# A two-layer decoder trunk on one core: SBUF homes at set distances modulo 512 bytes, and another order for the first stage

## The chip, the cores and the metric

The kernel runs on one core of a Trainium2 chip. The metric is device time in microseconds of one execution. Three runs of the kernel before took 998.0, 998.24 and 998.68 us.

## The reference

The input x is 256 positions by 1,024 channels, c is a conditioning vector, all in float32. Two layers, each of three residual sub-layers, and a final RMSNorm:

```python
def modnorm(x, g, shift, scale):
    return rmsnorm(x, g) * (1 + scale[:, None, :]) + shift[:, None, :]
def swiglu(h, w_gate, w_up, w_down):
    return (jax.nn.silu(h @ w_gate) * (h @ w_up)) @ w_down
c_act = jax.nn.silu(c)
for l in range(DEPTH):
    mod = (c_act @ w_mod[l] + b_mod[l]).reshape(B, N_SUB, 3, D_MODEL)
    shift, scale, gate = mod[:, :, 0], mod[:, :, 1], mod[:, :, 2]
    h = modnorm(x, norm_g[l, 0], shift[:, 0], scale[:, 0])
    x = x + 0.5 * gate[:, 0, None, :] * swiglu(h, w_ffn_gate[l, 0], w_ffn_up[l, 0], w_ffn_down[l, 0])
    h = modnorm(x, norm_g[l, 1], shift[:, 1], scale[:, 1])
    y = even_mixer(...) if l % 2 == 0 else odd_mixer(...)
    x = x + gate[:, 1, None, :] * y
    h = modnorm(x, norm_g[l, 2], shift[:, 2], scale[:, 2])
    x = x + 0.5 * gate[:, 2, None, :] * swiglu(h, w_ffn_gate[l, 1], w_ffn_up[l, 1], w_ffn_down[l, 1])
return rmsnorm(x, final_g)
```

The inner width of a SwiGLU is 2,816. The even mixer is a pooling mixer beside differential attention, the odd one a chunkwise mLSTM; each sits between one projection in and one out.

## The kernel before

Channels lie on the 128 partitions, so x is eight tiles `x[k]` of 128 x 256. All projections together are 2,560 units. A unit is one 128 x 128 block of a weight matrix times one 128 x 256 tile. For accuracy each weight block is split into a rounded high part `wh` and the rest `wl`, and each tile into a high and a low part. So a unit is three matmuls in a row (mm3, lines 341 to 343): `wh` with the high part, `wl` with the high part, `wh` with the low part.

**The weight stream.** SP loads chunks of 16 units (1 MB, `raww`) into five buffers that it shares with chunks `rawm` of the modulation matrix. For every half chunk ACT makes `wh` (line 299) and DVE makes `wl` by subtraction (line 300); four buffers each of `wh` and `wl`. A `rawm` chunk is read by DVE alone: `mod_sums` (line 267) multiplies it with silu(c) (`cact`) and sums along the row, two instructions of 128 x 1,024 a chunk. SP may load into a raw buffer again when DVE has read it.

**The moving operands** are three sets of tiles. In the first FFN, and for the first ten blocks of each later projection in, it is `xh[k]`/`xl[k]` (in the latter 258 columns, as two columns carry the shift); else `xs[k]`, the normed x. In the projections down and out it is a pair of tiles `hid`.

**The homes.** A tile's home is its address within the partition. The pools lay tiles one behind the other, each rounded up to 32 bytes. `xh`, `xl` and `hid` are 258 columns (1,032 bytes, so 1,056) and each next home lies 32 bytes further modulo 512; `xs` tiles are 1,024 bytes and all lie alike. Counted from the home of the weights (`wh` and `wl` all lie alike, a unit's columns at multiples of 512 bytes), modulo 512, worked out from the sizes: `xh[k]` at 320 + 32k, `xl[k]` at 64 + 32k, every `xs` at 320, the 46 `hid` slots at all sixteen multiples of 32.

**The first stage** (`first_ffn`, lines 526 to 597). DVE and ACT square the eight tiles, PE sums each over the partitions by matmuls with a column of ones (line 540), DVE makes the mean (`nv`, 543), POOL the power -1/2 (`nr`, 545), PE spreads it over the partitions (418). x times that (`hid`) is made by DVE for k = 0 (553) and by POOL for k = 1 to 7 (556). Then for each k the sixteen units of the first eight blocks follow (`START_BLOCKS`), for which DVE does the two modulation sums of k, the scale column (`acol`, 368), two `wl` and `xl[k]` (587), and ACT `xh[k]` (585) and a second copy in full precision (586). Behind its multiplications POOL makes masks and bands (`constants`, lines 208 to 235), which the mixers need later.

The order on each engine is made by a scheduler of the program, which takes instructions by when their inputs would be there; `issue_after` and `keep_in_program_order` bind single ones.

## Time and profile before

| | before |
|---|---|
| runs | 998.24 us median (998.0 to 998.68) |
| the profiled execution: time, span | 998.09 us, 996.4 us |
| PE busy, matmuls recorded | 973.5 us (98%), 8,032 |
| DVE, ACT, POOL busy | 758.1 us (76%), 528.0 us (53%), 217.9 us (22%) |
| DMA | 247.18 MB, mean 248 GB/s |
| granted clock, mean | 0.996 |

The span runs from the first to the last instruction. PE is matrix multiplication, PEld its weight loads, DVE, ACT and POOL the vector, scalar and general engines, SP the queue that issues the loads. Matmuls overlap in the pipeline, so their time is read from one start to the next and not from a record's length.

### The profile page before, as it was taken

To read this page: it belongs to the slowest core of one execution; us is meant where nothing else is said; L and a number is where in the kernel's file an instruction comes from. 1 tells how busy PE (TensorE), PEld (TensorE's weight loads), DVE (VectorE), ACT (ScalarE), POOL (GpSimd) and SP (SyncE) were. 2 spreads that over 40 slices of the span, in tenths; PEclk is the share of its full clock that TensorE was granted. 3 is DMA by queue.
4 is the path that set the end of the run, shared out by engine and by line. 5 is a ranking of instruction groups with operands and counts; after the bars stand their busy time and mean duration, and the time that the engine had idled before them with its cause. 6 is when DMAs were issued, how large, how long until landed. Compare 5 with 4: busy or idle time off the path is not lost.

```text
span 996.4 us, 19641 instructions
## 1 busy us (share of the span) xinstructions
PE 973.5 (98%) x8032; PEld 958.8 (96%) x8032; DVE 758.1 (76%) x1201; ACT 528.0 (53%) x872; POOL 217.9 (22%) x223
## 2 busy tenths in 40 slices
PE   7999999999999999999999999999999999999996
PEld 6899999999999999999999999999899999999996
DVE  5979998989879876777798676788867988555452
ACT  3475544448766544444465444445767655444441
POOL 4953220110112322211122222001010113222011
PEclk9999999999999999999999999999999999999998
DMA  9978888875846766766758766676565746565521
GB/s 341 317 295 318 328 329 319 341 284 206 298 155 246 271 245 254 277 252 235 290 182 291 288 245 248 269 293 258 200 223 185 280 171 244 205 229 175 187 105 43
DMA packets 36093, 247.18 MB, mean 248 GB/s; under 512 B 4001, under 2 KB 4385, under 8 KB 7458
## 3 DMA queue, kind: packets, MB, share of 16 engines
q1 hardware_dynamic: 35856, 245.81, 66.7%
q8 instruction: 63, 1.03, 0.4%
q14 instruction: 28, 0.23, 0.1%
q10 hardware_dynamic: 146, 0.11, 0.0%
HBM read 244.86 MB, written 1.05 MB: 247 GB/s over the span
## 4 chain that ended last, share of the span: by engine, by line
PE 82%; DVE 9%; ACT 3%; issue 3%; POOL 1%; DVEq 0%; ACTq 0%; POOLq 0%
PE one L343 26%; PE one L341 26%; PE one L342 26%; DVE wl L300 3%; DVE rawm L267 3%; ACT wh L299 1%; DVE xs L447 1%; POOL hr L401 1%; DVE xn L445 1%; PE one L418 0%; DVE xl L587 0%; DVE t L512 0%; DVE h L490 0%; ACT L488 0%; PE one L842 0%
## 5 line engine op out<-in xcount | busy, mean ns | idle before, releaser
L300 DVE TENSOR_TENSOR wl<-raww,wh 128x1024 fp32r<-128x1024 f32 x320 | 395.5, 1239 | 162.4 <-ACT wh L299 161.1
L299 ACT ACTIVATE wh<-raww 128x1024 fp32r<-128x1024 f32 x320 | 337.2, 1056 | 226.7 <-PE one L343 197.3
L341 PE MATMUL one<-xs,wh 128*128 128x256 f32 x976 | 275.3, 282 | 0.0
L342 PE MATMUL one<-xs,wl 128*128 128x256 f32 x976 | 272.9, 280 | 1.0 <-DVE wl L300 1.0
L343 PE MATMUL one<-xs,wh 128*128 128x256 f32 x976 | 273.1, 280 | 0.0
L341 PE MATMUL one<-hid,wh 128*128 128x256 f32 x832 | 233.7, 281 | 0.2 <-ACT hid L601 0.2
L343 PE MATMUL one<-hid,wh 128*128 128x256 f32 x832 | 233.7, 281 | 0.0
L342 PE MATMUL one<-hid,wl 128*128 128x256 f32 x832 | 233.3, 280 | 0.0
L342 PE MATMUL one<-xh,wl 128*128 128x258 f32 (+1 forms) x752 | 207.5, 285 | 3.2 <-DVE wl L300 2.9
L341 PE MATMUL one<-xh,wh 128*128 128x258 f32 (+1 forms) x752 | 208.1, 287 | 1.8 <-ACT xh L585 1.8
L343 PE MATMUL one<-xl,wh 128*128 128x258 f32 (+1 forms) x752 | 204.6, 283 | 0.0
L493 POOL TENSOR_TENSOR hid<-h,hid 128x256 fp32r<-128x256 f32 x88 | 123.3, 1402 | 340.1 <-ACT hid L492 340.1
L342 PEld LDWEIGHTS one<-xs,wl 128*128 128x128 f32 x976 | 183.6, 188 | 1.4 <-DVE wl L300 1.2
L341 PEld LDWEIGHTS one<-xs,wh 128*128 128x128 f32 x976 | 183.0, 187 | 1.2 <-issue 1.0
L343 PEld LDWEIGHTS one<-xs,wh 128*128 128x128 f32 x976 | 183.1, 188 | 0.0
L341 PEld LDWEIGHTS one<-hid,wh 128*128 128x128 f32 x832 | 156.8, 188 | 0.4 <-ACT hid L601 0.4
L343 PEld LDWEIGHTS one<-hid,wh 128*128 128x128 f32 x832 | 156.6, 188 | 0.2 <-DVE hid L602 0.2
L342 PEld LDWEIGHTS one<-hid,wl 128*128 128x128 f32 x832 | 156.7, 188 | 0.0
L267 DVE CUSTOM_DVE_ANT_0 rawm<-rawm,cact,pk 128x1024 f32<-128x1024 f32 x112 | 150.5, 1371 | 0.0
L342 PEld LDWEIGHTS one<-xh,wl 128*128 128x128 f32 x752 | 140.6, 191 | 5.4 <-DVE wl L300 5.2
L341 PEld LDWEIGHTS one<-xh,wh 128*128 128x128 f32 x752 | 140.3, 191 | 4.1 <-ACT xh L585 2.3
L343 PEld LDWEIGHTS one<-xl,wh 128*128 128x128 f32 x752 | 138.8, 189 | 0.2 <-DVE xl L587 0.2
(222 smaller groups left out, 727.0 us busy)
## 6 DMA issues: line engine op xcount, KB each, us to landing
...
```

The costliest lines, as they stand in the source:

```text
L267: nc.vector.tensor_tensor_reduce(out=ri, in0=ri, in1=cact, scale=factor, scalar=first, op0=ALU.mult, op1=ALU.add, accum_out=modc[n // KT][ ...
L299: nc.scalar.activation(whs[i], src, AF.Copy)
L300: ins = nc.vector.tensor_tensor(out=wls[i], in0=src, in1=whs[i].bitcast(F32), op=ALU.subtract)
L341: nc.tensor.matmul(out, lhsT=wh, rhs=rh, start=start, stop=False, skip_group_check=skip)
L342: nc.tensor.matmul(out, lhsT=wl, rhs=rh, start=False, stop=False, skip_group_check=skip)
L343: nc.tensor.matmul(out, lhsT=wh, rhs=rl, start=False, stop=stop, skip_group_check=skip)
L401: nc.gpsimd.tensor_tensor(out=r, in0=v, in1=mhalf[:, 0:width], op=ALU.pow)
L445: nc.vector.scalar_tensor_tensor(out=xn, in0=x[k], scalar=a, in1=r, op0=ALU.mult, op1=ALU.mult)
L447: nc.vector.scalar_tensor_tensor(out=to[1], in0=xn, scalar=b, in1=to[0].bitcast(F32), op0=ALU.add, op1=ALU.subtract)
L493: nc.gpsimd.tensor_tensor(out=hl[:, 0:T], in0=h, in1=hh[:, 0:T].bitcast(F32), op=ALU.subtract)
```

## The change

- **Homes.** The hid slots are 256 columns wide and come from two pools of 23, one for high parts (`slots()` takes one of each) and one for low parts; other users take turns. Fillers and the order of the tiles set the homes: weights at 0 modulo 512, high parts (`xs[k][0]`, first pool) at 448, low parts (`xs[k][1]`, second pool) at 192, `xh`/`xl` at 128, 160, 384 and 416, with `xl[k]` like `xh[k]`. Two users that need more than 256 columns (`gr`, `cp` in the odd mixer) take a buffer of the tag `acc`.
- **The first FFN uses `xs`** in all its units, not `xh`/`xl`.
- **Sums.** DVE squares k = 0, 1, 4 and ACT the other five; DVE adds them up in two sums of four; PE does four matmuls with ones instead of sixteen.
- **Order.** One modulation sum of k = 0 goes ahead of the mean, the other behind a copy of POOL's result. x times its norm goes from POOL to DVE in all k, with the scale in the same instruction; ACT makes only the high part (bias), DVE the low part. The matmuls of k = 0 go by operand: sixteen with `wh`, sixteen with `wl`, sixteen with the low part.
- **Matmuls of ones.** 21 matmuls of 128 x 256 whose result nobody reads: 8 ahead of the sums, 2 and 7 behind them, 4 behind the spreading. One SiLU of one column goes ahead on ACT.
- **POOL's constants** go piece by piece, from k = 0 on, bound only behind the power. The load of `pk2` stands behind them; `ghalf`, `gc` and `hg` are made behind the last x of the first stage.

```diff
+CONST_BASE = 16512
+RAW_PHASE, HIGH_PHASE, LOW_PHASE = 128, 448, 192
+SKIP = 192
...
-    hid = ctx.enter_context(tc.tile_pool(name="hid", bufs=46))
     tmp = ctx.enter_context(tc.tile_pool(name="tmp", bufs=2))
     small = ctx.enter_context(tc.tile_pool(name="small", bufs=2))
+    skip = ctx.enter_context(tc.tile_pool(name="skip", bufs=1))
+    hids = [ctx.enter_context(tc.tile_pool(name="hid0", bufs=23))]
+    skip2 = ctx.enter_context(tc.tile_pool(name="skip2", bufs=1))
+    hids.append(ctx.enter_context(tc.tile_pool(name="hid1", bufs=23)))
...
-    def slot(dt=F32):
-        return hid.tile([P, XC], dt, tag="hid", name=nm("hid"))
+    turn = [0]
+
+    def slot(dt=F32, i=None):
+
+        if i is None:
+            i = turn[0] = 1 - turn[0]
+        return hids[i].tile([P, T], dt, tag="hid", name=nm("hid"))
+
+    def slots():
+        return slot(F32R, 0), slot(F32R, 1)
...
+    modc, xh, xl = [], [], []
+    for i in range(2 * KT):
+        if i % 2 == 0:
+            up_to(RAW_PHASE, 256)
+        (xh if i < KT else xl).append(fixed(f"x{i}", XC, F32R))
+        if i % 2 == 1 and len(modc) < DEPTH * NSUB * 3:
+            modc += [fixed(f"mod{len(modc) + j}", KT) for j in range(6)]
+    mhalf = fixed("mhalf", 2)
+    wgh = fixed("wgh", 64, F32R)
+    up_to(HIGH_PHASE, 512)
+    xs = [[fixed(f"xs{k}", T, F32R)] for k in range(KT)]
+    wgl = fixed("wgl", 64, F32R)
+    up_to(LOW_PHASE, 512)
+    for k in range(KT):
+        xs[k].append(fixed(f"xs{k}l", T, F32R))
+    pk = fixed("pk", NPACK)
...
+    up_to(0, 512)
+    fill(skip, SKIP, "skip")
+    fill(skip2, (LOW_PHASE - HIGH_PHASE) % 512, "skip2")
...
+    onesr = xs[KT - 1][1]
+    nc.vector.tensor_copy(onesr, ones[:, 0:1].broadcast_to([P, T]))
+    junk = scol("junk", 1)
+    nc.scalar.activation(junk, ones[:, 0:1], AF.Silu)
+    warm = one()
+
+    def warm_up(n):
+
+        for _ in range(n):
+            tc.keep_in_program_order(nc.tensor.matmul(warm[:, 0:T], lhsT=onesr[:, 0:P], rhs=onesr, start=True,
+                                                         stop=True))
...
+    def constants_lane(behind):
+        for i, piece in enumerate(constants()):
+            with tc.issue_after(behind):
+                piece()
+            if i % 2:
+                yield 4
         nc.sync.dma_start(pk2, pack2)
+        yield 64
...
-        hh, hl = slot(F32R), slot(F32R)
+        hh, hl = slots()
...
+        acc, sq = [slot()[:, 0:T] for _ in range(2)], [slot()[:, 0:T] for _ in range(KT)]
+        for k in range(KT):
+            to = acc[0] if k == 0 else acc[1] if k == 4 else sq[k]
+            if k in (2, 3, 5, 6, 7):
+                nc.scalar.activation(to, x[k], AF.Square)
+            else:
+                nc.vector.tensor_tensor(out=to, in0=x[k], in1=x[k], op=ALU.mult)
+            if k % 4:
+                last = nc.vector.tensor_tensor(out=acc[k // 4], in0=acc[k // 4], in1=to, op=ALU.add)
+                tc.keep_in_program_order(last)
+        warm_up(8)
         pss = one()
-        for k in range(KT):
-            sq = slot()
-            if k in (5, 6, 7):
-                nc.scalar.activation(sq[:, 0:T], x[k], AF.Square)
-            else:
-                nc.vector.tensor_tensor(out=sq[:, 0:T], in0=x[k], in1=x[k], op=ALU.mult)
+        for j, v in enumerate(acc):
             for i in range(2):
-                nc.tensor.matmul(pss[:, i:i + 1], lhsT=sq[:, i * P:(i + 1) * P], rhs=ones[:, 0:1],
-                                 start=k == 0 and i == 0, stop=k == KT - 1, skip_group_check=True)
+                tc.keep_in_program_order(
+                    nc.tensor.matmul(pss[:, i:i + 1], lhsT=v[:, i * P:(i + 1) * P], rhs=ones[:, 0:1],
+                                     start=j == 0 and i == 0, stop=j == 1, skip_group_check=True))
+            warm_up((2, 7)[j])
         v = scol("nv", 2)
+        with tc.issue_after(last.ins):
+            mod_sums(0, 1)
         nv = nc.vector.tensor_scalar(out=v, in0=pss[:, 0:2], scalar1=1.0 / D, scalar2=EPS, op0=ALU.mult, op1=ALU.add)
+        tc.keep_in_program_order(nv)
         stat["rcol"] = scol("nr", 2)
-        nc.gpsimd.tensor_tensor(out=stat["rcol"], in0=v, in1=mhalf, op=ALU.pow)
-        with tc.issue_after(nv.ins):
+        pw = nc.gpsimd.tensor_tensor(out=stat["rcol"], in0=v, in1=mhalf, op=ALU.pow)
+        after = nc.vector.tensor_copy(scol("after", 2), stat["rcol"])
+        tc.keep_in_program_order(after)
+        with tc.issue_after(after.ins):
             mod_sums(0)
-            nc.vector.tensor_scalar(out=ghalf, in0=pcol("b_mod", 0, 144), scalar1=0.5, scalar2=None, op0=ALU.mult)
         psb = stats_bcast()
-        for k in range(KT):
-            xn.append(slot()[:, 0:T])
-            if k == 0:
-                nc.vector.tensor_tensor(out=xn[k], in0=x[k], in1=psb, op=ALU.mult)
-                nc.scalar.activation(rext[:, 0:T], psb, AF.Copy)
-            else:
-                last = nc.gpsimd.tensor_tensor(out=xn[k], in0=x[k], in1=rext[:, 0:T], op=ALU.mult)
+        warm_up(4)
...
-            nc.scalar.activation(xh[k][:, 0:T], xn[k], AF.Identity, bias=b, scale=a)
-            nc.scalar.activation(xn[k], xn[k], AF.Identity, bias=b, scale=a)
-            nc.vector.tensor_tensor(out=xl[k][:, 0:T], in0=xn[k], in1=xh[k][:, 0:T].bitcast(F32), op=ALU.subtract)
+            xn.append(slot()[:, 0:T])
+            if k == 0:
+                for i in range(2):
+                    high(i)
+            xi = nc.vector.scalar_tensor_tensor(out=xn[k], in0=x[k], scalar=a, in1=psb if k == 0 else rext[:, 0:T],
+                                                op0=ALU.mult, op1=ALU.mult)
+            xc = nc.scalar.activation(xs[k][0], xn[k], AF.Identity, bias=b)
+            if k == 0:
+                tc.keep_in_program_order(xc)
+                tc.keep_in_program_order(nc.scalar.activation(rext[:, 0:T], psb, AF.Copy))
+                with tc.issue_after(xi.ins):
+                    split_to(1)
+            nc.vector.scalar_tensor_tensor(out=xs[k][1], in0=xn[k], scalar=b, in1=xs[k][0].bitcast(F32),
+                                           op0=ALU.add, op1=ALU.subtract)
             split_to(((k + 1) * nb - 1) // HALF_UNITS)
+            if k == 0:
+                ws = [(out(b), unit(), b) for b, _ in order[0:nb]]
+                for j in range(3):
+                    for o, (wh, wl), b in ws:
+                        tc.keep_in_program_order(
+                            nc.tensor.matmul(o, lhsT=wl if j == 1 else wh, rhs=xs[0][j // 2],
+                                             start=j == 0 and b[1] == 0, stop=False, skip_group_check=True))
+                spawn(constants_lane(pw.ins))
+                continue
             for b, _ in order[k * nb:(k + 1) * nb]:
-                mm3(out(b), (xh[k][:, 0:T], xl[k][:, 0:T]), k == 0 and b[1] == 0, k == KT - 1, True)
+                mm3(out(b), xs[k], False, k == KT - 1, True)
                 if k == KT - 1:
                     done(b)
         look[0] = 2
-        with tc.issue_after(last.ins):
-            constants()
-        gemm(order[KT * nb:], range(KT), lambda k: (xh[k][:, 0:T], xl[k][:, 0:T]), out, done)
+        with tc.issue_after(xi.ins):
+            nc.vector.tensor_scalar(out=ghalf, in0=pcol("b_mod", 0, 144), scalar1=0.5, scalar2=None, op0=ALU.mult)
+            nc.vector.tensor_scalar(out=gc, in0=pcol("subln_g"), scalar1=1.0 - LAMBDA_INIT, scalar2=None, op0=ALU.mult)
+            nc.vector.tensor_scalar(out=hg, in0=pcol("mlstm_g", 0, 8), scalar1=0.5, scalar2=None, op0=ALU.mult)
+        gemm(order[KT * nb:], range(KT), lambda k: xs[k], out, done)
...
-            gr = slot()
+            gr = tmp.tile([P, XC], F32, tag="acc", name=nm("gr"))
...
-            cp = slot()
+            cp = tmp.tile([P, XC], F32, tag="acc", name=nm("cp"))
```

**DVE from the mean to the first weights.** `nv` is the mean, `rawm`/`mod` a modulation sum, `hid` x times its norm, `acol` the scale column, `wl` the low weights. Before:

```order
L543 TENSOR_SCALAR nv_202<-one_169 128x2 [waits PE_49]
L267 ISA rawm_163,mod_120<-rawm_163,cact,pk 128x1024 [waits DMAHW4_49,Activation_49]
L267 ISA mod_120 128x1
L267 ISA rawm_163,mod_121<-rawm_163,cact,pk 128x1024 [waits DMAHW5_49]
L267 ISA mod_121 128x1
L548 TENSOR_SCALAR ghalf<-pk 128x144
L553 TENSOR_TENSOR hid_212<-xa,one_209 128x256 [waits PE_49]
L368 SCALAR_TENSOR_TENSOR acol_229<-mod_121,pk 128x1 [waits DVE_49]
L300 TENSOR_TENSOR wl_235<-raww_166,wh_234 128x1024 [waits DMAHW6_49,Activation_49]
```

Now:

```order
L340 ISA rawm_186,mod_90<-rawm_186,cact,pk 128x1024 [waits DMAHW4_49,DMAHW2_49]
L340 ISA mod_90 128x1
L632 TENSOR_SCALAR nv_238<-one_224 128x2 [waits PE_49]
L636 COPY after_243<-nr_241 128x2 [waits Pool_49]
L340 ISA rawm_186,mod_91<-rawm_186,cact,pk 128x1024 [waits DMAHW5_49]
L340 ISA mod_91 128x1
L447 SCALAR_TENSOR_TENSOR acol_253<-mod_91,pk 128x1 [waits DVE_49]
L674 SCALAR_TENSOR_TENSOR hid_255<-xa,acol_253,one_246 128x256 [waits DVE_49,PE_49]
L379 TENSOR_TENSOR wl_263<-raww_189,wh_256 128x1024 [waits DMAHW6_49,Activation_49]
```

One sum moved ahead of `nv`; the other waits for POOL's power (through the copy), and `hid` now waits for `acol`, as the scale is in it.

**DVE in one k of the first stage**, here from `acol` of k = 1 to the next sum. Before:

```order
L368 SCALAR_TENSOR_TENSOR acol_229<-mod_121,pk 128x1 [waits DVE_49]
L300 TENSOR_TENSOR wl_310<-raww_302,wh_309 128x1024 [waits DMAHW1_49,Activation_49]
L300 TENSOR_TENSOR wl_314<-raww_302,wh_313 128x1024 [waits DMAHW2_49,Activation_49]
L587 TENSOR_TENSOR xl_92<-hid_215,xh_84 128x256 [waits Activation_49]
L267 ISA rawm_365,mod_120<-rawm_365,cact,pk 128x1024 [waits DMAHW3_49]
```

Now:

```order
L447 SCALAR_TENSOR_TENSOR acol_253<-mod_91,pk 128x1 [waits DVE_49]
L379 TENSOR_TENSOR wl_343<-raww_333,wh_341 128x1024 [waits DMAHW1_49,Activation_49]
L674 SCALAR_TENSOR_TENSOR hid_337<-xa,acol_253,rext 128x256 [waits DVE_49]
L379 TENSOR_TENSOR wl_347<-raww_333,wh_345 128x1024 [waits DMAHW2_49,Activation_49]
L682 SCALAR_TENSOR_TENSOR xs1l<-hid_337,mod_90,xs_130 128x256 [waits Activation_49]
L340 ISA rawm_407,mod_90<-rawm_407,cact,pk 128x1024 [waits DMAHW3_49]
```

DVE has one instruction more, `hid`, and it stands behind the first `wl`. Not seen here: on ACT both `wh` of a k now stand ahead of its high part, where before the high part stood between them.

**POOL behind the power** (`nr`). Before:

```order
L545 TENSOR_TENSOR nr_204<-nv_202,mhalf 128x2 [waits DVE_49]
L556 TENSOR_TENSOR hid_215<-xa,rext 128x256 [waits DMAHW1_49,Activation_49]
L556 TENSOR_TENSOR hid_217<-xa,rext 128x256
L556 TENSOR_TENSOR hid_219<-xa,rext 128x256
L556 TENSOR_TENSOR hid_221<-xa,rext 128x256 [waits DMAHW3_49]
L556 TENSOR_TENSOR hid_223<-xa,rext 128x256
L556 TENSOR_TENSOR hid_225<-xa,rext 128x256
L556 TENSOR_TENSOR hid_227<-xa,rext 128x256
L210 MEMSET m_831 128x384
```

Now:

```order
L635 TENSOR_TENSOR nr_241<-nv_238,mhalf 128x2 [waits DVE_49]
L275 MEMSET m_324 128x384
L281 CAST identr<-ident 128x128 [waits Pool_49]
L277 AFFINE_SELECT m_324<-m_324 128x128 [waits Pool_49]
L277 AFFINE_SELECT m_324<-m_324 128x128
```

The seven multiplications are gone, and the pieces of the constants follow the power in the same order as before, with no other work of POOL between them.

## Rows read from the trace of the kernel before

**Rows 1.** The page, part 1: engine, busy us (share of the span), instructions.

```profile
PE 973.5 (98%) x8032; PEld 958.8 (96%) x8032; DVE 758.1 (76%) x1201; ACT 528.0 (53%) x872; POOL 217.9 (22%) x223
```

**Rows 2.** Busy us of engines by stretch, clock granted, DMA share, GB/s.

```profile
0.00:25.00 25.00, 19.20 (x86) 16.12 (x87) 13.07 (x27) 7.70 (x12) 10.21 (x13) 1.00 0.90 340
25.00:50.00 25.00, 23.76 (x186) 22.50 (x186) 23.02 (x34) 11.98 (x16) 25.00 (x41) 1.00 0.93 319
100.00:200.00 100.00, 100.00 (x849) 100.00 (x849) 89.08 (x134) 48.39 (x67) 17.40 (x15) 1.00 0.86 330
```

**Rows 3.** The timeline to the first units: start us, us, engine, line, operation [idle before].

```profile
5.02 1.43 DVE L538 TENSOR_TENSOR hid<-xa 128x256 f32<-128x256 f32 x4 [3.82 <-DMA xa<-xT]
...
5.99 6.99 PE L540 MATMUL one<-ones,hid 128*128 128x1 f32 x32
...
6.59 1.02 ACT L536 ACTIVATE hid<-xa 128x256 f32<-128x256 f32 x3
...
13.01 0.16 DVE L543 TENSOR_SCALAR nv<-one 128x2 f32<-128x2 f32 x1 [5.78 <-PE one L540]
...
13.26 1.73 POOL L545 TENSOR_TENSOR nr<-nv,mhalf 128x2 f32<-128x2 f32 x1 [11.89 <-DVE nv L543]
...
16.30 0.42 DVE L553 TENSOR_TENSOR hid<-xa,one 128x256 f32<-128x256 f32 x1 [0.51 <-PE one L418]
...
17.68 1.01 PE L341 MATMUL one<-xh,wh 128*128 128x256 f32 x3 [1.42 <-ACT xh L585]
```

**Rows 4.** The same timeline: POOL, and a DVE sum beside it.

```profile
17.22 9.66 POOL L556 TENSOR_TENSOR hid<-xa,rext 128x256 f32<-128x256 f32 x7 [2.23 <-ACT rext L554]
...
21.09 1.75 DVE L267 CUSTOM_DVE_ANT_0 rawm<-rawm,cact,pk 128x1024 f32<-128x1024 f32 x1
...
26.82 0.41 POOL L210 MEMSET m<- 128x384 f32 x1
...
56.24 1.92 POOL L232 TENSOR_TENSOR band<-band,ident 128x128 f32<-128x128 f32 x2
```

**Rows 5.** The timeline of the first stage at k = 1 and around k = 7.

```profile
24.57 0.58 DVE L368 SCALAR_TENSOR_TENSOR acol<-mod,pk 128x1 f32<-128x1 f32 x1
...
25.24 0.60 ACT L585 ACTIVATE xh<-hid,mod,acol 128x256 fp32r<-128x256 f32 x1 [5.23 <-DVE acol L368]
...
25.90 0.38 PE L341 MATMUL one<-xh,wh 128*128 128x256 f32 x1 [0.43 <-ACT xh L585]
...
57.96 1.28 DVE L300 TENSOR_TENSOR wl<-raww,wh 128x1024 fp32r<-128x1024 f32 x1 [0.55 <-ACT wh L299]
59.16 0.45 DVE L587 TENSOR_TENSOR xl<-hid,xh 128x256 fp32r<-128x256 f32 x1
59.54 1.34 DVE L267 CUSTOM_DVE_ANT_0 rawm<-rawm,cact,pk 128x1024 f32<-128x1024 f32 x1
...
62.13 0.16 DVE L368 SCALAR_TENSOR_TENSOR acol<-mod,pk 128x1 f32<-128x1 f32 x1
...
63.73 0.52 PE L341 MATMUL one<-xh,wh 128*128 128x256 f32 x3
```

**Rows 6.** PE alone by stretch: length, busy us (matmuls that reach into it), clock, DMA.

```profile
332.93:428.69 95.76, 95.76 (x815) 1.00 0.72 268
428.80:491.02 62.22, 62.22 (x530) 1.00 0.67 254
73.91:150.23 76.32, 76.32 (x647) 1.00 0.85 323
310.70:331.31 20.61, 20.61 (x174) 1.00 0.58 204
47.50:50.33 2.83, 2.83 (x26) 1.00 1.04 405
34.93:40.08 5.15, 5.15 (x44) 1.00 0.98 366
```

**Rows 7.** PE's timeline at a unit with `xh[4]` in the first FFN.

```profile
94.97 0.28 PE L341 MATMUL one<-xh,wh 128*128 128x256 f32 x1
...
95.32 0.28 PE L341 MATMUL one<-xh,wh 128*128 128x256 f32 x1
```

More of the change, by code (lines that the diff above doesn't have):

```diff
@@ L188, in pcol @@
+    identr = fixed("identr", P, F32R)
+    maskT = fixed("maskT", P)
+    tri = fixed("tri", P)
+    band = fixed("band", len(WINDOWS) * 3 * P, shape=[P, len(WINDOWS), 3 * P])
+    up_to(0, 512)
+    fill(skip, SKIP, "skip")
+    fill(skip2, (LOW_PHASE - HIGH_PHASE) % 512, "skip2")
     def pcol(n, i=0, w=1):
@@ L270, in mod_sums @@
                 mod_ready[n] = True
+            if sums is not None:
+                return
     mod_ready = {}
@@ L637, in even_mixer @@
         lamc = scol("lamc", 4)
-        gc = scol("gc")
         parts, vT, ys = {}, {}, {}
```

111 lines of the change are left out of this document (59 added, 52 removed).

## The prediction

> **What bounds the kernel now.** I read the page first: PE is busy 98% of the span [rows 1]. That alone doesn't say that PE is the limit everywhere, so the stretches come next. From 100 us on PE never pauses: 100.00 of 100 us, at full clock, with DVE at 89% and the loads at 330 GB/s [rows 2]. There only two things can shorten the run: fewer matmuls, or a shorter time from one matmul's start to the next. In the first 50 us it is otherwise: PE starts its first unit at 17.68 [rows 3], and from then to the end of the first stage it pauses for others. So the run is the time until PE no longer waits, plus about 7,700 matmuls at their spacing, plus what the mixers and the tail cost, which the change leaves alone.
>
> *Who holds PE in the first stage.* Up to the first unit it is a chain: squares from 5.02, 32 passes of PE with a column of ones that take 6.99 us, the mean at 13.01, POOL's power for 1.73, the spreading, x times it at 16.30, ACT, and PE at 17.68 [rows 3]. Then every k is one lap of DVE. `acol` stands at 24.57 for k = 1 and at 62.13 for k = 7 [rows 5]: six laps in 37.56 us, 6.26 each, in which DVE is busy 92% [rows 2]. PE needs 48 matmuls x 0.118 = 5.65 us a lap, so DVE, not PE, sets the pace. What DVE idles in a lap, it waits for ACT's `wh` (0.55 us) [rows 5]. The loads reach 319 to 340 GB/s there [rows 2]; SP's next load waits for a buffer that DVE gives back, so it follows DVE.
>
> *The spacing.* Taking off the one or two matmuls that reach into a stretch from before it, rows 6 give, in ns from start to start: `xs` 95.76 us over 813 = 117.8; `hid` 62.22 over 527 = 118.1; `xh`/`xl` in the first FFN 76.32 over 645 = 118.3; those of 258 columns 20.61 over 172 = 119.8. In the first stage, where one k holds for 48 matmuls, the home alone makes a difference: k = 4 (high part 448 from the weights' home, low part 192) runs 24 in 2.82 us = 117.7, and k = 2 (384 and 128) 43 in 5.15 us = 119.8 [rows 6]. Same instructions, same shapes, clock 1.00 in both. So the home matters, and the new homes of `xs` and `hid` are those of k = 4.
>
> **The change, part by part.**
>
> *The mean.* DVE now has three squares and six additions, nine instructions of 1.43/4 = 0.36 us from 5.02 [rows 3], so 8.2 if none waits. ACT did three squares from 6.59 in 1.02 us [rows 3] and now has about as much there with one SiLU between; with that the last addition ends near 8.7. The four matmuls are eight passes of 6.99/32 = 0.22, four of them behind the last sum: 9.6. One modulation sum now stands ahead of the mean on DVE (1.27, [rows 5]: 59.54 to the next less half): 10.0. So the mean is at 10.0 where it was at 13.01.
>
> *To the first unit.* From the mean to POOL's result there were 1.98 us [rows 3], so it stands at 12.0. The spreading is over by 13.3 (16.30 - 13.01 = 3.29 behind the mean). DVE waits for POOL with the copy, and what queues behind it is the second sum: 0.15 + 1.27, then `acol` and `hid`: 13.9. ACT's high part takes 0.60 [rows 5]. First matmul at 14.6, against 17.68. The 21 matmuls of ones are covered by PE's waits: eight before 8.7, nine in POOL's power, four from 13.3. At 0.3 us each (three in 1.01 at 17.68, [rows 3]) the four end at 14.5; were they slower, they would cost up to 0.5. The clock column says 1.00 all along, though the first matmuls stand further apart than later ones; I count nothing for the clock, as the lap of k = 0 hangs on DVE.
>
> *To k = 1.* Two `wl` at 1.20 (57.96 to 59.16), the low part 0.38, the two sums and `acol` 2.59 (59.54 to 62.13) [rows 5]: `acol` of k = 1 at 19.3. Beside POOL's multiplications a sum took 1.75 instead of 1.34 [rows 4, 5]; these are gone, but POOL's constants now run here, so I take 19.3 to 20.1. Then one `wl`, `hid` and ACT: 2.2 us, where it was 1.33 (24.57 to 25.90). First matmul of k = 1 near 22.0, against 25.90 [rows 5].
>
> *The laps.* DVE: two `wl` 2.40, `hid` 0.38 (new), low part 0.38, sums and `acol` 2.59, together 5.75, with no wait for ACT, as both `wh` now stand ahead of the x in ACT's order. The constants took POOL from 26.82 to about 58 [rows 4], beside these same laps; now they begin at 12 and reach to about 44. Bounds for a lap: 5.75 with POOL silent, 6.26 as it was. I take 5.95, nearer the lower, as the last two laps are free of POOL. Six laps: 35.7, so k = 7 begins at 57.7 instead of 63.73 [rows 5], 6.0 us earlier; the bounds give 4 to 7.6. At the end of the stage `wl` and the low part of k = 7 come later behind `acol` than before: I take off 0.5. **Term: -5.5 us (-4 to -7).** SP's loads of a lap move earlier with DVE. The load of `pk2` (0.4 MB) goes behind two weight loads; its first reader is at the stage's end, so it costs nothing. The moved `ghalf`, `gc`, `hg` are three short DVE instructions in a stretch at the stage's end.
>
> *The homes.* `xs` (2,928 matmuls) has 117.8 and stays there: 0. `hid` (2,496): 118.1 to 117.8 = -0.75. The first FFN behind its first stage (672), now `xs`: 118.3 to 117.8 = -0.35. The 258 columns (1,200) get homes that the trace doesn't show as a pair. Bounds: 117.8 x 258/256 = 118.7, a gain of 1.3; the bad 119.8 x 258/256 = 120.7, a loss of 1.1. I take -1.2, the nearer row being the good homes of the other sets. **Term: -2.3 us (0 to -3).** Other uses of the slots only change hands; `gr` and `cp` share the two `acc` buffers, whose other users are a stage apart.
>
> *Sum.* The profiled execution took 998.1 (span 996.4 and 1.7 around it), 0.15 below the median. 998.1 - 5.5 - 2.3 = **990.3**.
>
> **The rivals.**
>
> *The new homes are faster than any steady stretch (977.6).* In the first FFN behind its stage, a unit with `xh[4]`, the very homes, takes 0.35 us [rows 7]; 29 of them average 347 ns, where three matmuls of the stretch average 354 to 355. If that held throughout: 2,160 units x 7 = -15, with the start 977.6. Against it: 24 in a row at these homes run at 117.7 [rows 6], and three sets with other homes level off at 117.8 to 118.1, so the short unit looks like time made up behind longer ones.
>
> *A steady bad home (1004).* Where homes vary, good and bad average out; fixed ones repeat the same meeting for ever. With `wh`, `wl`, `wh` in a row on high, high, low (in the first stage the order was another) the pattern might settle where k = 2 did: 6,480 x (119.8 - 118.0) = +11.7, less 5.5: 1004.3. It decides from 118.85 ns a matmul on, where it eats the whole 5.5. For it: rows 6 show such a level. Against it: the homes are those of the better one.
>
> *POOL against DVE (995.4).* The constants now run with no gap beside k = 0 to 4. If each sum and each `wl` of four laps cost 0.4 more, as the sum at 21.09 did [rows 4], the laps are 7.35: 22.4 + 4 x 7.35 + 2 x 5.75 = 63.3. The start gives 0.4, and with the homes 995.4. Against it: the same constants already stood beside laps of 6.26.
>
> *The homes do nothing (992.6).* Then only the start counts: 998.1 - 5.5 = 992.6. Against it stand 117.7 and 119.8 for the same work [rows 6]. The Trainium skill, page "SBUF — State Buffer", section "Who interferes with whom", says that PE and ACT never wait on anyone and that only the port pair of DVE and GpSimd is contended; by that no address could change PE's spacing, and this rival would be right. The two spacings speak against it, unless something else than SBUF makes them.
>
> **How the numbers follow.** Forecast 0.55, faster homes 0.17, POOL 0.12, homes nothing 0.08, bad home 0.08. About 0.2% (2 us) is what a measurement can tell from no change: faster is below 996.2. The forecast, the faster homes, the homes that do nothing and half of the POOL case are faster: 0.86; the other half of POOL the same: 0.06; the bad home slower: 0.08. The range goes from 979, which leaves out the fuller half of the faster homes, to 996, which holds the POOL case.
>
> **What would show it.** The mean near 10, the first unit near 14.6, k = 1 near 22, k = 7 near 58, laps of 5.75 to 6.1. The spacing 117.8 in `xs` and `hid` alike, 118.7 to 119.2 at 258 columns. Units of 347 ns through a whole stretch would prove the first rival, more than 118.85 a matmul the second; sums of 1.75 before 45 us the third. What would make it wrong: PE idle in mid-run, where DVE is at 89%.

## The result, and the profile after

The changed kernel took **970.63 us** (median of four runs, 969.95 to 973.11), the kernel before 998.21 beside it (998.0 to 998.68). The ratio is 0.9728, with a 95% interval of 0.9709 to 0.9746: 27.6 us faster, where 7.8 were forecast and 979 was the lower end of the range. The profiled execution took 970.05, its span is 968.3.

The page, part 1 (answers to [rows 1]), and the stretches (columns as in [rows 2]):

```profile
PE 948.1 (98%) x8029; PEld 933.9 (96%) x8029; DVE 760.8 (79%) x1214; ACT 525.0 (54%) x867; POOL 201.2 (21%) x216
```

```profile
0.00:25.00 25.00, 20.60 (x112) 17.21 (x113) 19.07 (x37) 11.66 (x18) 15.12 (x31) 1.00 0.93 364
25.00:50.00 25.00, 23.16 (x190) 22.14 (x189) 24.60 (x37) 9.64 (x12) 16.07 (x40) 1.00 0.97 361
100.00:200.00 100.00, 100.00 (x851) 100.00 (x851) 89.64 (x134) 48.52 (x66) 15.71 (x14) 1.00 0.87 328
```

The units are the same 7,680 matmuls as before, done in 25 us less of PE. Neither the first 50 us nor the stretch from 100 to 200 show that. Counting PE's matmuls of the type fp32r (those of the units and 32 in the mixers) in the two traces does. The table says when the N-th of them started:

| matmul | place | before, us | after, us | difference |
|---|---|---|---|---|
| 0 | first unit | 17.68 | 14.07 | -3.6 |
| 48 | k = 1 | 25.90 | 21.51 | -4.4 |
| 336 | k = 7 | 63.73 | 58.71 | -5.0 |
| 384 | behind the first stage | 69.59 | 64.46 | -5.1 |
| 1,584 | behind the first FFN | 212.54 | 206.05 | -6.5 |
| 2,400 | second FFN | 330.48 | 322.59 | -7.9 |
| 3,840 | behind the second FFN | 502.66 | 488.45 | -14.2 |
| 5,400 | behind the third FFN | 687.49 | 667.33 | -20.2 |
| 7,711 | the last | 984.95 | 956.92 | -28.0 |

So the first stage gave 5.1 us, about as forecast, and 23 us came later, little by little, in the FFNs. PE alone by stretch (columns as in [rows 6]) says how. In order: `xs` and `hid` of the first FFN, `xs` and `hid` of the second, `xs` of the third, 258 columns. Each stretch begins and ends at a matmul's start, so two of the matmuls counted (in some stretches three) reach into it from before:

```profile
76.61:143.74 67.13, 67.13 (x572) 1.00 0.88 335
144.10:205.81 61.71, 61.71 (x526) 1.00 0.85 320
326.35:417.01 90.66, 90.66 (x802) 1.00 0.75 275
418.03:476.74 58.71, 58.71 (x520) 1.00 0.70 261
508.57:599.23 90.66, 90.66 (x802) 1.00 0.76 280
304.06:322.46 18.40, 18.40 (x154) 1.00 0.57 208
```

67.13 us over 570 is 117.8 ns, and 61.71 over 524 the same. But 90.66 over 800 is **113.3**, and so is 58.71 over 518: same homes, same clock, same instructions. Behind its first stage the first FFN runs all along at 117.8, the later ones at 113.3, and none of these long stretches lies between. The 258 columns stand at 121.1, against 119.8 before [rows 6].

The spacing is settled where a run of matmuls begins, and then held. At 58.5 us PE pauses for 0.12 us, and behind the pause the spacing is another (two rows of PE's timeline ahead of it, two behind):

```profile
58.36 0.28 PE L421 MATMUL one<-xs,wl 128*128 128x256 f32 x1
58.48 0.28 PE L422 MATMUL one<-xs6l,wh 128*128 128x256 f32 x1
58.71 0.38 PE L420 MATMUL one<-xs,wh 128*128 128x256 f32 x1
58.93 0.28 PE L421 MATMUL one<-xs,wl 128*128 128x256 f32 x1
```

Ahead of it 113.3 (k = 6 from 53.3 us on), behind it 117.8 until 206 us. Not every pause turns it: one of 0.15 us at 76.0 us, in the same run, left it at 117.8. My expectations below call the lower spacing 113.5; that mean still held the first matmuls of each run.

The trace of before has the lower spacing too, in one place that I had not looked at: 16 matmuls of `xs` in the odd mixer, while its long stretches stand at 117.8:

```profile
719.32:721.02 1.70, 1.70 (x16) 1.00 0.55 154
521.09:616.84 95.75, 95.75 (x815) 1.00 0.74 269
```

1.70 over 15 is 113.3, 95.75 over 813 is 117.8. So 117.8 was never a floor.

### The profile page after: what moved, and what is told of

It reads as the page before. It is cut to its first block, busy times and chain, and to the rows that moved or that the text cites. A ratio compares the mean times of both kernels' runs of the same rounds, so it can differ in the third digit from the quotient of the medians.

```text
span 968.3 us, 19626 instructions
## 1 busy us (share of the span) xinstructions
PE 948.1 (98%) x8029; PEld 933.9 (96%) x8029; DVE 760.8 (79%) x1214; ACT 525.0 (54%) x867; POOL 201.2 (21%) x216
## 4 chain that ended last, share of the span: by engine, by line
PE 85%; DVE 8%; issue 2%; ACT 2%; DMA 1%; POOL 1%; SPq 0%; DVEq 0%; ACTq 0%; POOLq 0%
PE one L420 27%; PE one L422 27%; PE one L421 27%; DVE wl L379 3%; DVE rawm L340 2%; DMA raww<-wst 1%; ACT wh L362 1%; DVE xn L524 1%; POOL hr L480 1%; DVE t L591 0%; PE one L497 0%; DVE hid L674 0%; PE one L768 0%; PE one L766 0%; PE one L944 0%
## 5 line engine op out<-in xcount | busy, mean ns | idle before, releaser
L420 PE MATMUL one<-xs,wh 128*128 128x256 f32 x1312 | 366.5, 280 | 3.6 <-ACT xs L676 3.5
L421 PE MATMUL one<-xs,wl 128*128 128x256 f32 x1312 | 362.8, 278 | 0.8 <-DVE wl L379 0.8
L420 PEld LDWEIGHTS one<-xs,wh 128*128 128x128 f32 x1312 | 246.7, 188 | 6.0 <-ACT xs L676 4.7
L421 PEld LDWEIGHTS one<-xs,wl 128*128 128x128 f32 x1312 | 247.4, 189 | 1.4 <-DVE wl L379 1.2
L572 POOL TENSOR_TENSOR hid<-h,hid 128x256 fp32r<-128x256 f32 x88 | 120.6, 1373 | 344.1 <-ACT hid L571 344.1
L420 PE MATMUL one<-x,wh 128*128 128x258 f32 x400 | 115.8, 290 | 0.0
L421 PE MATMUL one<-x,wl 128*128 128x258 f32 x400 | 112.9, 282 | 1.1 <-DVE wl L379 1.1
L422 PE MATMUL one<-x,wh 128*128 128x258 f32 x400 | 113.6, 284 | 0.0
L464 POOL TENSOR_TENSOR acc<-acc,sq 128x256 f32<-128x256 f32 x41 | 35.0, 854 | 261.5 <-ACT sq L460 238.1
L420 PEld LDWEIGHTS one<-x,wh 128*128 128x128 f32 x400 | 76.3, 191 | 1.7 <-issue 1.3
L421 PEld LDWEIGHTS one<-x,wl 128*128 128x128 f32 x400 | 76.4, 191 | 1.3 <-DVE wl L379 1.3
L422 PEld LDWEIGHTS one<-x,wh 128*128 128x128 f32 x400 | 76.0, 190 | 0.3 <-DVE x L471 0.2
L567 ACT ACTIVATE sg<-one 128x256 f32<-128x256 f32 x73 | 27.8, 384 | 79.6 <-PE one L422 79.4
```

Of the source, the lines that this page charges most:

```text
L420: nc.tensor.matmul(out, lhsT=wh, rhs=rh, start=start, stop=False, skip_group_check=skip)
L421: nc.tensor.matmul(out, lhsT=wl, rhs=rh, start=False, stop=False, skip_group_check=skip)
L422: nc.tensor.matmul(out, lhsT=wh, rhs=rl, start=False, stop=stop, skip_group_check=skip)
L464: eng.tensor_tensor(out=stat["acc"], in0=stat["acc"], in1=sq, op=ALU.add)
L567: nc.scalar.activation(sg, gate, AF.Silu, bias=bias_g)
L572: nc.gpsimd.tensor_tensor(out=hl[:, 0:T], in0=h, in1=hh[:, 0:T].bitcast(F32), op=ALU.subtract)
```

## The experiments

**Each half alone.** e1 takes the homes back:

```diff
-    hids = [ctx.enter_context(tc.tile_pool(name="hid0", bufs=23))]
-    hids.append(ctx.enter_context(tc.tile_pool(name="hid1", bufs=23)))
+    hid = ctx.enter_context(tc.tile_pool(name="hid", bufs=46))
...
-                mm3(out(b), xs[k], False, k == KT - 1, True)
+                mm3(out(b), (xh[k][:, 0:T], xl[k][:, 0:T]), False, k == KT - 1, True)
```

> The changed kernel with the homes, the tile widths and the tiles of the first FFN as before; only the first stage is new. Theory (two spacings): the trace after shows only two spacings at the new homes, 113.5 and 117.8 ns, each held for hundreds of matmuls; the gain behind the first stage is the lower one. By that the new first stage alone gives what it gave by the start of matmul 384, 69.59 - 64.46 = 5.1 us, so about 993, and xs stands at 117.8 as before. Rival (the start sets it): the entry into the run, not the homes, decides which spacing holds; then xs shows 113.5 here too and the time is 975 to 985.

e2 puts only the pools, the fillers and `xs` in the first FFN into the kernel before:

```diff
+    hids = [ctx.enter_context(tc.tile_pool(name="hid0", bufs=23))]
+    hids.append(ctx.enter_context(tc.tile_pool(name="hid1", bufs=23)))
...
-                mm3(out(b), (xh[k][:, 0:T], xl[k][:, 0:T]), k == 0 and b[1] == 0, k == KT - 1, True)
+                mm3(out(b), xs[k], k == 0 and b[1] == 0, k == KT - 1, True)
```

> The kernel before with the new homes and the first FFN on xs; its first stage is as it was. Theory (two spacings): the homes admit the lower spacing, and it appears in most long stretches of xs and hid: -15 to -25 us, 973 to 983, and each stretch shows either 113.5 or 117.8 and nothing between. My prediction's term (homes to a floor of 117.8): -2.3, 996. Rival (the start sets it): 117.8 throughout, 993 to 996.

e1: 992.1 beside 997.8, ratio 0.9945 (0.9928 to 0.9961), so -5.5 us (-3.9 to -7.2) for the first stage. e2: 972.8, ratio 0.9751 (0.9737 to 0.9766), so -24.8 us for the homes. PE alone, `xs` of the third FFN in e1, then `xs` and `hid` of the first FFN in e2:

```profile
515.04:610.80 95.76, 95.76 (x816) 1.00 0.73 268
```

```profile
75.11:147.19 72.08, 72.08 (x638) 1.00 0.91 337
148.10:206.92 58.82, 58.82 (x522) 1.00 0.87 334
```

117.8 without the homes; 113.3 with them (72.08 over 636, 58.82 over 519), here in the first FFN also, beside the same loads. So the two parts add up to more than the change, 30.3 us against 27.6: after spends its first FFN at 117.8, 1,200 x 4.44 ns = 5.3 us. That is more than the 2.7 us that are to be explained; 0.9 of the rest is the odd mixer's `hid`, which stood at 117.8 in e2, and what remains is no more than the intervals of the three runs leave open.

**Which homes.** e3 sets high and low of `xs` and `hid` all at 320, from the weights, the old home of `xs`:

```diff
-RAW_PHASE, HIGH_PHASE, LOW_PHASE = 128, 448, 192
+RAW_PHASE, HIGH_PHASE, LOW_PHASE = 128, 320, 320
+HID_HIGH, HID_LOW = 320, 320
```

> The changed kernel with high and low parts of xs and hid all at 320 from the weights, the home that xs had before. Theory (the distance decides): xs and hid at 117.8 nearly everywhere, so 4,700 matmuls lose 4.25 ns each, +20 us, about 991. Rival (it is enough that the homes do not vary, any distance will do): the lower spacing appears as after, 970 to 975, in hid too.

e3 took 989.3, ratio 0.992 (0.9905 to 0.9935). PE alone, `xs` of the third FFN and `hid` of the even mixer:

```profile
513.54:608.59 95.05, 95.05 (x809) 1.00 0.74 270
274.51:293.10 18.59, 18.59 (x166) 1.00 0.41 150
```

117.8 in nearly all stretches, so the distance matters and not only that homes are alike. But one run of 176 took 113.3 (18.59 over 164): at 320 it can be held, and is rarely entered. e14 and e15 are edits of the same two lines:

```diff
+RAW_PHASE, HIGH_PHASE, LOW_PHASE = 128, 384, 128
+HID_HIGH, HID_LOW = 0, 256
```

> The changed kernel with xs at 384/128 and hid at 0/256, no extra matmuls. Theory (the pair decides which spacings there are): xs at 119 ns, as hid stood at these homes in e8, so 3,500 matmuls lose 4.5 to 5 ns against after, about +16 us; hid unknown, 113.5 or 117.8. Rival (the entry decides; 119 in e8 came from the extra matmuls): xs at 113.5 or 117.8 here.

```diff
+RAW_PHASE, HIGH_PHASE, LOW_PHASE = 128, 64, 320
+HID_HIGH, HID_LOW = 192, 192
```

> The changed kernel with xs at 64/320 (the homes before had 320 in both) and hid at 192/192. Theory (the pair decides; one part at 320 is enough to hold 117.8): xs at 117.8 in all long stretches, hid at 113.5 where it enters so. Rival (the entry decides): xs at 113.5 in the later three FFNs as after.

e14, with the whole new first stage in it, took **999.7**, ratio 1.0031 (1.0018 to 1.0044): 0.3% slower than before. e15 took 986.9 in its one run. PE alone, e14: `xs` of the second and third FFN, `hid` of the third; e15: `xs` of the third, `hid` of the first:

```profile
328.06:423.94 95.88, 95.88 (x810) 1.00 0.72 265
518.11:614.95 96.84, 96.84 (x810) 1.00 0.73 266
616.02:676.98 60.96, 60.96 (x510) 1.00 0.69 263
```

```profile
511.60:606.52 94.92, 94.92 (x808) 1.00 0.73 270
144.02:203.29 59.27, 59.27 (x525) 1.00 0.86 331
```

384/128 stands at 118.7 or 120.0, 0/256 at 120.0 (60.96 over 508), 64/320 at 117.8, and 192/192 at 113.3 in the first FFN and 117.8 in the later ones. The homes decide which spacings there are.

No run moved the weights while the moving tiles stayed, so whether the distance from the weights counts or a tile's own address is argued. The two layouts bear on it: by the sizes the weights lie at 416 modulo 512 in the kernel before and at 0 in the changed one. At the distances 320/320 both hold 117.8, and at 384/128 the kernel before shows 119.8 (k = 2 of its first stage) and e14 118.7 to 120.0, though the tiles' own addresses differ by 416. That speaks for the distance.

**The spacing as a state.** e4, e7 and e8 put one more matmul of 32 to 256 columns ahead of each output block; e7 has other homes beside it (`xs` 320/320, `hid` 448/448), e8 too (`xs` 192/448, `hid` 384/128):

```diff
+            if k == ks[0]:
+                kick(out(b), r[0])
...
+        w = (32, 64, 96, 128, 160, 192, 224, 256)[kicks[0] % 8]
...
+        nc.tensor.matmul(o[:, 0:w], lhsT=whs[h][:, 0:P], rhs=r[:, 0:w], start=True, stop=True)
```

> The changed kernel with one more matmul ahead of each output block's first, of 32 to 256 columns in turn, into the same bank (it is overwritten by the block's first matmul, so it adds work only). Theory (the spacing is a state that a disturbance can set anew): the spacing changes between 113.5 and 117.8 at some of the extra matmuls, always at once and for the whole block, and which one follows depends on the number of columns. Rival (the spacing is set by what else runs at the time, DVE or loads in the first FFN): the first FFN stays at 117.8 and the later ones at 113.5, whatever is put between. The time itself is not compared: about 160 more matmuls.

> As e4 (an extra matmul of 32 to 256 columns ahead of each block), with xs at 320/320 and hid at 448/448. Theory (both spacings exist at every fixed pair of homes, the pair only changes which one an entry leads to): after some of the extra matmuls blocks at 113.5 and others at 117.8 in both sets, in other shares than in e4. Rival (the difference of 256 bytes between high and low makes the lower spacing): no block at 113.5 in either set.

> As e4, with xs at 192/448 (high and low exchanged) and hid at 384/128, the homes of k = 2 in the first stage of before, where 43 matmuls took 119.8 each. Theory (state at every fixed pair): 113.5 and 117.8 in both sets, and nothing at 119.8, which was the first stage's order. Rival (the distances set the value): hid at 119 to 120, xs as in e4.

PE alone in e4, 16 matmuls in each of eight blocks in a row in the first FFN, behind extra matmuls of 32, 64, 96, 128, 160, 192, 224 and 256 columns:

```profile
87.55:89.44 1.89, 1.89 (x19) 1.00 0.99 390
90.49:92.37 1.88, 1.88 (x18) 1.00 1.16 410
93.43:95.25 1.82, 1.82 (x18) 1.00 0.97 396
96.28:98.17 1.89, 1.89 (x19) 1.00 1.02 412
99.22:101.11 1.89, 1.89 (x19) 1.00 1.09 407
102.16:103.98 1.82, 1.82 (x18) 1.00 0.97 387
105.00:106.81 1.81, 1.81 (x18) 1.00 1.09 398
107.83:109.65 1.82, 1.82 (x19) 1.00 1.05 410
```

1.89 us is 118 ns a matmul, 1.82 is 114. So it turns at the extra matmuls, in the first FFN too, with DVE and the loads as they were; the rival falls. Over the whole trace of e4, a matmul of 128 columns turned the spacing each time (14 times up, 11 times down), one of 256 never (23 times). That holds for the homes 448/192, and 128 columns turn 192/448 too (18 of 18 in `xs` of e8); but at 320/320 they left 117.8 as it was in 18 of 18 places (`xs` of e7). Blocks of 256 columns in the three traces, by the spacing they held:

| homes, high/low | 113.3 | 117.8 | 118.5 to 120 | between |
|---|---|---|---|---|
| `xs` 448/192 (e4) | 62 | 79 | 0 | 4 |
| `hid` 448/192 (e4) | 14 | 29 | 0 | 0 |
| `xs` 192/448 (e8) | 54 | 87 | 0 | 4 |
| `hid` 448/448 (e7) | 16 | 27 | 0 | 0 |
| `xs` 320/320 (e7) | 1 | 144 | 0 | 0 |
| `hid` 384/128 (e8) | 0 | 1 | 42 | 0 |

The old home of `xs` hardly ever comes down, the homes of k = 2 in the first stage of before never, and all three others do. My theory of e7 and e8, that every fixed pair has both, falls. The rival of e7, that a difference of 256 bytes makes the lower spacing, falls with 448/448, and with 384/128 and 0/256.

**Can it be set?** e5 puts 192 columns ahead of the first four blocks behind the stage, e9 128 columns ahead of the eleventh:

```diff
+                nc.tensor.matmul(out(b)[:, 0:192], lhsT=unit_peek(), rhs=r[0][:, 0:192], start=True, stop=True)
```

> The changed kernel with four more matmuls of 192 columns, one ahead of each of the first four output blocks behind the first stage, into a bank that the block's first matmul overwrites. In e4 a matmul of 192 columns turned 117.8 into 113.5 in 10 of 16 places and left 113.5 alone. Theory (the spacing is a state): the 1,200 matmuls of the first FFN behind the stage, at 117.8 after, run at 113.5 from the first or second of the four on: -5.1 us, plus 4 x 0.11 of added work, so about 966. Rival (DVE or the loads hold PE in the first FFN): 117.8 there as after, 971.

> The changed kernel with one more matmul, of 128 columns, ahead of the eleventh output block behind the first stage (near 92 us, behind PE's last short wait for wl at 76 and 81.7 us, where the run of e5 fell back to 117.8). Theory (a state, set anew by a disturbance; in e4 a matmul of 128 columns turned 117.8 into 113.5 in 11 of 11 places): 113.5 from 92 to 205 us, 960 matmuls x 4.25 = -4.1 us, so 966.5, in every run that came there at 117.8. Rival (something in the first FFN keeps it at 117.8, whatever stands before): 970.6.

e5 took 969.3 (965.2 to 971.3), e9 967.1 (966.2 to 971.1), both with intervals that overlap the change's. PE alone in e5 and in e9, behind the extra matmuls, then later:

```profile
77.10:81.29 4.19, 4.19 (x39) 1.00 0.66 209
83.03:142.98 59.95, 59.95 (x512) 1.00 0.90 345
```

```profile
88.56:92.30 3.74, 3.74 (x35) 1.00 0.94 370
94.05:142.93 48.88, 48.88 (x418) 1.00 0.91 339
```

In e5 the lower spacing was there until a pause of 0.1 us at 81.7 sent it up again. In e9 the run stayed at 113.3 through such a pause at 81.9, and the 128 columns at 92.6 turned it up, for 4 us lost. Its five runs fall into 966.2 to 967.1 and 970.6 to 971.1, which fits a matmul that turns whatever it finds. So the spacing can be turned on purpose, but not set without knowing it.

**The first stage.** e6 leaves the matmuls of ones out, e10 starts POOL's constants behind the last k:

```diff
-        for _ in range(n):
+        for _ in range(0):
```

> The changed kernel without its 21 matmuls of ones. My prediction's step: they lie in PE's waits, and the lap of k = 0 hangs on DVE, so the time moves by less than 0.5 us, except where the first FFN enters the other spacing. Rival (they keep PE's clock up): without them the first 48 matmuls stand 0.2 to 0.4 us apart, as before, with k = 0 at least 5 us longer on PE; DVE's lap of k = 0 ends near 21, so the time grows by 2 to 5 us.

```diff
-                spawn(constants_lane(pw.ins))
...
+        spawn(constants_lane(xi.ins))
```

> The changed kernel with POOL's constants begun only behind the first stage, as before, still in small pieces. My prediction's step: with POOL silent a lap of DVE is 5.75 instead of 5.95 for four laps, so k = 7 begins 0.8 us earlier, and nothing is lost later: 970. Rival (the constants cost DVE nothing beside it, as the laps of after show): the same within 0.3 us at the start of k = 7.

e6: 970.6, ratio 0.9758 (0.9725 to 0.979), the same. PE's timeline at k = 0 and k = 1 in e6:

```profile
14.04 3.63 PE L690 MATMUL one<-xs,wh 128*128 128x256 f32 x16 [1.51 <-ACT xs L676]
17.50 1.99 PE L690 MATMUL one<-xs,wl 128*128 128x256 f32 x16
...
21.48 0.38 PE L420 MATMUL one<-xs,wh 128*128 128x256 f32 x1 [0.18 <-ACT xs L676]
```

Without ones the first sixteen take 3.63 us instead of 2.09; but k = 1 comes at 21.48, as after (21.51), since it hangs on DVE. The ones speed PE where nobody waits for it.

The granted clock reads 1.00 there, but at the start of a trace that column misleads. The first sixteen of e6 start 0.21 us apart. In e16 (below) PE has the same 0.21 us from start to start, behind a stop, at a granted clock of 0.50, the lower level of 1.2 GHz:

```profile
96.00:98.00 2.00, 2.00 (x11) 0.50 0.75 221
```

The trace of e6 holds no entry for the clock before 17.34 us, just where its matmuls come closer together; that of the kernel before has its first at 21.43, where its slow ones end. Time without an entry is shown as 1.00. So without ones the first sixteen most likely ran at the lower level, and with them (2.09 us) at the higher.

e10 took 965.8 (964.9 to 970.3). It did not do what its expectation says: `issue_after` sets an order, no wait, and with POOL idle the constants ran in one piece from 11.3 to 34.5. So it says little of them. In its profiled execution the first FFN stood at 113.3, which makes the gain there; its interval (0.9669 to 0.9732) overlaps the change's. e16 holds them with a copy that reads the last x; e17 is e16 with e11's homes:

```diff
+        hold = nc.gpsimd.tensor_copy(scol("hold", 2), xs[KT - 1][0][:, 0:2].bitcast(F32))
+        tc.keep_in_program_order(hold)
+        spawn(constants_lane(hold.ins))
```

> The changed kernel with POOL's constants truly held back: a POOL copy that reads the last x of the first stage stands ahead of them, so that POOL is silent beside all laps (in e10 they ran at once from 11.3 to 34.5 us, since the order set no wait). Theory (POOL beside DVE lengthens a lap from 5.68, as the two last laps of after, to 6.2 to 6.9): six laps of 5.68, so k = 7 begins near 55.3 instead of 58.7, and the end moves by up to -3.4 us, less what the constants then cost beside the wl of 65 to 100 us; 967 to 970, and 4 us less where the first FFN takes 113.5. Rival (the laps are long for the loads, which the wl wait for at 320 GB/s and more, not for POOL): k = 7 at 58 to 59 as after.

> e16 and the 258-column tiles at 0, 32, 256 and 288 (e11) together. Theory (independent parts): the lap gain of e16 and -1.4 us, so 966 to 969 with the first FFN at 117.8 and 962 to 965 with it at 113.5. Rival (what is won in the first stage is lost behind it): 969 to 970.

DVE's timeline, the start of each lap (`acol`), after: four laps beside the constants, two with POOL silent; then e16, the first and the last lap:

```profile
18.95 0.16 DVE L447 SCALAR_TENSOR_TENSOR acol<-mod,pk 128x1 f32<-128x1 f32 x1
25.52 0.23 DVE L447 SCALAR_TENSOR_TENSOR acol<-mod,pk 128x1 f32<-128x1 f32 x1
...
38.85 0.23 DVE L447 SCALAR_TENSOR_TENSOR acol<-mod,pk 128x1 f32<-128x1 f32 x1
45.05 0.16 DVE L447 SCALAR_TENSOR_TENSOR acol<-mod,pk 128x1 f32<-128x1 f32 x1
50.73 0.16 DVE L447 SCALAR_TENSOR_TENSOR acol<-mod,pk 128x1 f32<-128x1 f32 x1
56.41 0.16 DVE L447 SCALAR_TENSOR_TENSOR acol<-mod,pk 128x1 f32<-128x1 f32 x1
```

```profile
18.56 0.16 DVE L447 SCALAR_TENSOR_TENSOR acol<-mod,pk 128x1 f32<-128x1 f32 x1
24.24 0.16 DVE L447 SCALAR_TENSOR_TENSOR acol<-mod,pk 128x1 f32<-128x1 f32 x1
...
47.38 0.16 DVE L447 SCALAR_TENSOR_TENSOR acol<-mod,pk 128x1 f32<-128x1 f32 x1
53.06 0.16 DVE L447 SCALAR_TENSOR_TENSOR acol<-mod,pk 128x1 f32<-128x1 f32 x1
```

5.68 with POOL silent, 6.2 to 6.9 beside its constants. In e16 five of six laps are 5.68, and matmul 384 starts at 61.1 instead of 64.5: 3.3 us. Its k = 7 starts at 55.4, near the 55.3 of the theory, so it was POOL that lengthened the laps, and the rival that named the loads (58 to 59) falls. Yet e16 took 983.4 and e17 985.8. Two things ate it. POOL now had hid's low parts behind 24 us of constants; the waits of e16 from 60 to 110 us, and the stretch with PE's pause:

```profile
DVE h L569 <- POOL hid L572: 10.4, 6, 6.7
...
PE one L421 <- DVE wl L379: 2.8, 1, 2.8
```

```profile
90.00:100.00 10.00, 7.22 (x49) 7.02 (x48) 6.52 (x9) 2.98 (x5) 5.44 (x25) 0.83 0.35 120
```

DVE waited for POOL, `wl` came late, and PE stood for 2.8 us; behind the stop it ran at a granted clock of 0.50 (the row of 96 to 98 us above), so that the whole stretch shows 0.83. And the new small tile moved both pools of `hid` by 64 bytes, from 448/192 to 0/256. PE alone, `hid` of the first FFN in e16:

```profile
144.54:205.98 61.44, 61.44 (x515) 1.00 0.86 327
```

120.0 (61.44 over 512), as e14 shows for that pair: against 113.3, 2,496 x 6.67 = 16.6 us, for 64 bytes. Against after it is 14.3, as the first of its five stretches of `hid` stood at 117.8.

**The 258 columns, and the best of all.** e11 and e12 move the tiles of 258 columns, e11 with `RAW_PHASE` 0, e12 with 64:

```diff
-RAW_PHASE, HIGH_PHASE, LOW_PHASE = 128, 448, 192
+RAW_PHASE, HIGH_PHASE, LOW_PHASE = 0, 448, 192
```

> The changed kernel with the tiles of 258 columns at 0, 32, 256 and 288 instead of 128, 160, 384 and 416. The trace of before gives 357 ns for a unit with x at 0/256 and 360 at 32/288, that of after 362 at its homes. Theory (the home sets the value): -3.5 ns in 400 units, -1.4 us, 969. Rival (258 columns have one value, whatever the home): 120.6 a matmul, no change.

> As e11, with 64, 96, 320 and 352; by the trace of before 359 (320/64) and 362 (352/96) a unit. Theory (the home sets the value): -1 to 0 us. Rival (one value): 120.6 a matmul.

e11: 970.5; its 258 columns take 119.5 on average instead of 120.6, 1.3 us for an expected 1.4, but too little to see in the time, where other stretches took the higher spacing. e12: 966.6 (966.2 to 967.5), with 120.4 there; in its profiled execution the first FFN stood at 113.3, which makes the gain there, and its interval (0.9675 to 0.9717) overlaps the change's. e13 (e10, e11 and three times 192 columns) and e18 (e16 and e11 with both faults mended: homes back, constants one by one between the low parts of hid) were meant to beat the change:

```diff
+            tc.keep_in_program_order(piece())
...
+        tc.keep_in_program_order(
+            nc.gpsimd.tensor_tensor(out=hl[:, 0:T], in0=h, in1=hh[:, 0:T].bitcast(F32), op=ALU.subtract))
```

> The changed kernel with POOL's constants behind the first stage (e10), the 258-column tiles at 0, 32, 256 and 288 (e11) and one more matmul of 192 columns ahead of the output blocks 11, 13 and 15 behind the first stage (in e4 and e5 192 columns never turned 113.5 into 117.8, and turned 117.8 into 113.5 in 10 of 16 places). Theory (the spacing is a state; the three parts add): start -0.8, 258 columns -1.4, the first FFN from 92 us on at 113.5 in most runs, -4.1, plus 3 x 0.11: 970.6 - 6.0 = 964.6. Rival (the first FFN's spacing falls as it will, whatever stands before): runs at both 964.5 and 968.7.

> e17 mended in its two faults: hid is back at 448/192 (in e16 and e17 a new small tile had moved the two pools by 64 bytes, to 0/256, the homes that stood at 120 in e14), and POOL's constants go piece by piece between the low parts of hid, in program order, from about 92 us on instead of in one piece from 68.7 to 92.7, where they held hid, then DVE, then PE. The 258-column tiles stay at 0, 32, 256 and 288. Theory (independent parts): stage end at 61.1 as in e16, 3.35 us before after's; -1.4 for the 258 columns; so 965.9 with the first FFN at 117.8 and 961.8 with it at 113.5. Rival (the constants cost DVE and then PE as much behind the stage as beside it): 969 and 965.

e13 took 965.9 (962.9 to 973.0), e18 969.7 (961.7 to 973.4). In the trace of e13 the first of the three extra matmuls left 117.8 as it was, the second turned it to 113.3, and there it stayed (31.80 us over 270 ahead, 35.82 over 316 behind). The profiled execution of e18 took 961.65, where its theory had 961.8 with the lower spacing (matmul 384 at 61.0, first FFN at 113.3). But the other five stand between 966.6 and 973.4, and neither interval (0.9671 to 0.9734 and 0.9715 to 0.9772) leaves the change's. The 11.7 us between runs of one kernel are about two FFNs at one spacing or the other (5.3 for the first, 1,344 x 4.44 = 6.0 for a later one); only the profiled executions were traced, so that is argued.

## Why the prediction was wrong

The direction was right, the size was not. By its steps:

- **The mean and the first unit: right.** 10.34 for 10.0. From there POOL's result took 0.98 instead of the 1.98 I carried over, and the first unit came at 14.07 for 14.6. k = 1 at 21.51 for 22.0. The rows, with [rows 3] before:

```profile
10.34 0.15 DVE L632 TENSOR_SCALAR nv<-one 128x2 f32<-128x2 f32 x1
10.58 0.70 POOL L635 TENSOR_TENSOR nr<-nv,mhalf 128x2 f32<-128x2 f32 x1 [9.21 <-DVE nv L632]
11.32 0.35 DVE L636 COPY after<-nr 128x2 f32<-128x2 f32 x1 [0.82 <-POOL nr L635]
```

- **The laps: the size was off.** I took 5.95 between 5.75 and 6.26. The lower bound is real (5.68 with POOL silent), but beside the constants a lap is 6.5, not 6.05: (45.05 - 18.95)/4. So six laps took 37.46, as before (37.56, from [rows 5]), and the whole gain in the stage came from its start. My rival "POOL against DVE" had the mechanism, at half its price. It did not decide, as the earlier k = 1 stood against it: DVE began the laps 5.6 us earlier (18.95 for 24.57), where I had 4.5 to 5.3, and the laps gave 0.1 us where I had 1.9. The term came to -5.1 by the trace and -5.5 by e1, for -5.5; that it came so close is in part luck.
- **"`xs` has 117.8 and stays there: 0": this step failed.** I read 117.7 from 24 matmuls in a row at the new homes [rows 6], saw three sets level off at 117.8 to 118.1, and called it a floor. It is the upper of two spacings that these homes have. `xs` in the three later FFNs: 2,448 x 4.44 = 10.9 us; `hid` behind the first FFN: 1,968 x (118.1 - 113.3) = 9.4, where I had 0.75 for all of it. In the first FFN, at 117.8, the step held: 1,200 matmuls took 141.59 us for 142.95. So the term of the homes, put at -2.3, measured some -23 by the trace and -24.8 in e2.
- **The rival "faster than any steady stretch" is what happened**, with a chance of 0.17. It pointed at these very homes, by units of 347 ns at `xh[4]` [rows 7], and I talked it away as time made up behind longer units. Whether those units were a sign of the lower spacing is not shown: 347 is neither 340.0 nor 353.3. A steady unit takes 340.0 now; the two products above, 20.3 us, came of it where I had 15. So the rival was right in direction and had neither the two levels nor the size.
- **The rival "a steady bad home" exists**, at other homes: e14 stands at 118.7 to 120.0 and is slower than before with the whole first stage gained, near its price of 1004 (999.7). Its reason fits in part: fixed homes do hold one spacing for hundreds of matmuls, but at 448/192 either of two.
- **The 258 columns:** 121.1 in the long stretch for 118.8; a loss of a microsecond at most where I had -1.2.
- **The homes that do nothing** would have been 992.6. The Trainium skill, page "SBUF — State Buffer", section "Who interferes with whom", has PE wait on no one. Here PE's spacing goes from 113.3 (after) to 120.0 (e14) with nothing changed but addresses. So the measurement decides against what I drew from it, that no address could change the spacing; whether PE waits for anything there is not shown.

What stays open: what in the chip ties PE's spacing to the homes, and why a run of matmuls begins at one spacing or the other. The first FFN ended at 117.8 in after, e5, e6 and e11 and at 113.3 in e2, e10, e12 and e18.
